# Up projection: five of 22 channel tiles from seven products of summed quarters, alternating with plain tiles

## The chip, the cores and the metric

One Trainium2 chip, and one of its cores. The metric is the device time of one execution in microseconds, the median of several runs of the same kernel.

## The reference, cut to what matters

A decoder layer: three attention branches are mixed and projected, and a gated MLP with a short convolution over positions follows. The change lies in the MLP's up projection alone.

```python
h = rmsnorm(x, norm_ffn_pre[l])                       # 512 tokens x 1024
u = causal_depthwise_conv(h @ w_ffn_up[l], ffn_conv_w[l], ffn_conv_b[l])   # 1024 x 5632
u_gate, u_val = jnp.split(u, 2, axis=-1)              # 2816 channels each
y = (jax.nn.gelu(u_gate, approximate=True) * u_val) @ w_ffn_down[l]
x = x + rmsnorm(y, norm_ffn_post[l])
```

Everything is float32. The kernel keeps that precision by splitting each operand into a high part and a low part in a rounded float32 format, and by three matmuls for each product (high x high, high x low, low x high).

## The kernel before, in words

The up projection makes 44 tiles of 128 channels x 512 tokens: for each f from 0 to 21 a gate tile (number 2f) and a value tile (number 2f+1). One tile is a sum over 8 slices of 128 inputs, and each slice takes the three matmuls of mm3 (lines 127 to 130), so a tile is 24 matmuls with 512 columns of moving data. The moving operands are h1h and h1l, the high and low parts of the normalized input, which stay in memory for the whole stage; the stationary operands are the weights.

Weights come in pieces of 128 partitions x 1024 values, one piece for a tile. issue (line 95) has SyncE load a piece into a raw buffer (line 103; four of them) and split (lines 81 to 88) makes its two parts: ScalarE copies raw to whi (line 84), and VectorE subtracts whi from raw to make wlo (line 85). There are three buffers each for whi and wlo; the loop asks for the piece of tile i+2 when tile i begins.

Each finished tile lies in a PSUM bank. conv (line 805) reads it three times: once on ScalarE (line 808) and twice on VectorE (lines 809 and 810), into one of four c buffers. The gate tile then goes through Gelu on ScalarE (line 822), and GpSimd multiplies gate and value (line 829). The down projection that follows already works with seven products of sums for 20 of the 22 tiles; after every fourth f sums (lines 783 to 790) makes its sums on GpSimd.

TensorE's instructions keep the order of the program. The other engines' order is set by a planner that simulates the program when it is built and gives an engine whichever instruction is ready, the earlier one of the program first; on the chip each engine then works through its list in that order. The four tiles 0 to 3 are begun early on half of the tokens (256 columns), which is why the trace of before has this shape too.

Of the kernel before, what the change touches and what calls it, by code (L numbers as in the profile page):

```python
# [11 lines left out]
F32 = mybir.dt.float32  # L12
F32R = mybir.dt.float32r
AF = mybir.ActivationFunctionType
ALU = mybir.AluOpType
# [4 lines left out]
P = 128  # L20
# [10 lines left out]
EARLY = 4  # L31
NG = 5
NS = 4 * NG
C_QMB, C_KMB, C_VMB, C_QSW, C_KSW, C_QME = 0, 512, 1024, 1536, 2048, 2304
C_GMB, C_GSW, C_GME = 2816, 3840, 4864

# [2 lines left out]
def tile_hybrid_layer(  # L39
# [24 lines left out]
    def T(pool_, shape, dt, tag, bufs=None):  # L64
        count[0] += 1
        kw = {} if bufs is None else {"bufs": bufs}
        return pool_.tile(shape, dt, tag=tag, name=f"{tag}_{count[0]}", **kw)

    def PT(tag):
        return T(pp, [P, 512], F32, tag, {"pj": 2, "s": 3, "t": 2, "o": 1}[tag])  # L70
# [24 lines left out]
    def issue(upto):  # L95

        while issued[0] <= min(upto, len(stream) - 1):
            i = issued[0]
            src, into = stream[i]
            k, c = src.shape[0] // P, src.shape[1]  # L100
            raw = T(wp, [P, 1024], F32, "raw", 4)
            view = raw[:].rearrange("p (k c) -> p k c", k=k)
            sp.dma_start(view, src.rearrange("(k p) c -> p k c", p=P))
            if into is None:
                dst = [(T(wp, [P, 1024], F32R, "whi", 3)[:], T(wp, [P, 1024], F32R, "wlo", 3)[:])]
            else:
                dst = into()
            hi, lo = [], []
            n = max(1, k // len(dst))
            for j, (a, b) in enumerate(dst):  # L110
                a3, b3 = (w.rearrange("p (k c) -> p k c", k=n) for w in (a, b))
                part = view[:, j * n : (j + 1) * n, :] if k > 1 else view[:, :, j * c // len(dst) : (j + 1) * c // len(dst)]
                split(a3, b3, part, eng=pool if i in on_pool else dve)
                hi += [a3[:, q, :] for q in range(n)]
                lo += [b3[:, q, :] for q in range(n)]
            units[i] = (hi, lo)
            issued[0] += 1
# [5 lines left out]
    def unit(i, ahead=2):  # L123
        issue(i + ahead)
        return units[i]
# [85 lines left out]
    def up_block(i, into=None):  # L211
        c = i // 2 + NF * (i % 2)
        b_up[i] = block(w_ffn_up[0][:, c * P : (c + 1) * P], into)
# [6 lines left out]
    up_block(0, lambda: [tuple(T(mp, [P, 1280], F32R, "P", 2)[:, 0:1024] for _ in range(2))])  # L220
    up_block(1, lambda: [tuple(T(ap, [P, 512], F32R, "pt", 5)[:] for _ in range(2)) for _ in range(2)])
    for i in range(2, 2 * NF):
        up_block(i)
    on_pool.update(b_mem[:3] + b_up[:3])


# [544 lines left out]
    fp = ctx.enter_context(tc.tile_pool(name="fp", bufs=2))  # L771
    c_tile = lambda: T(fp, [P, 512], F32, "c", 4)
    c_next = [c_tile()]
    gpair = [T(fp, [P, 4, 2, 256], F32, "G", NG) for _ in range(NG)]
    gsum = [[t[:, i, :] for i in range(3)] for t in (T(fp, [P, 3, 512], F32, "S", NG - 1) for _ in range(NG - 1))]
    gsum.append([T(mp, [P, 512], F32, "o", 3)[:] for _ in range(3)])
    grest = T(fp, [P, NF - NS, SEQ], F32, "gN", 1)

    def quarters(d):

# [11 lines left out]
    def up_products(i):  # L792

        if i in early:
            ps, u = early[i]
            a = 256
        else:
            u = unit(b_up[i])
            ps = PT("t" if i < EARLY + 2 else "pj")
            a = 0  # L800
        for k in range(KD):
            mm3(ps[:, a:512], u[0][k], u[1][k], h1h[:, k, a:512], h1l[:, k, a:512], k == 0, k == KD - 1)
            yield ps

    def conv(i, ps):
        ch = i // 2 + NF * (i % 2)
        c = c_next.pop() if c_next else c_tile()
        act.activation(c[:], ps[:], AF.Identity, scale=convw[:, 88 + ch : 89 + ch], bias=convw[:, 132 + ch : 133 + ch])  # L808
        dve.scalar_tensor_tensor(c[:, 1:512], ps[:, 0:511], convw[:, 44 + ch : 45 + ch], c[:, 1:512], op0=ALU.mult, op1=ALU.add)  # L809
        dve.scalar_tensor_tensor(c[:, 2:512], ps[:, 0:510], convw[:, ch : ch + 1], c[:, 2:512], op0=ALU.mult, op1=ALU.add)  # L810
        return c

    for f in range(NF):
        if f == 0:
            for k, banks in enumerate(zip(up_products(0), up_products(1))):
                if k + 4 < KD:
                    turn1(k + 4)
            issue(b_up[EARLY + 1])
        else:
            banks = [list(up_products(2 * f))[-1]]  # L820
        cg = conv(2 * f, banks[0])
        act.activation(cg[:], cg[:], AF.Gelu_apprx_tanh)  # L822
        if f:
            banks.append(list(up_products(2 * f + 1))[-1])
            issue(b_up[min(2 * f + 3, 2 * NF - 1)])
        cv = conv(2 * f + 1, banks[1])
        if f < NS:
            halves2 = lambda ap: ap.rearrange("p (c n) -> p c n", c=2)
            pool.tensor_tensor(gpair[f // 4][:, f % 2 :: 2, f % 4 // 2, :], halves2(cg[:]), halves2(cv[:]), op=ALU.mult)  # L829
        else:  # L830
            pool.tensor_tensor(grest[:, f - NS, :], cg[:], cv[:], op=ALU.mult)
        if f < NS and f % 4 == 3:
            sums(f // 4)

    gffn = [T(fp, [P, 512], F32, "gffn", 2) for _ in range(2)]
    for h in range(2):
# [198 lines left out]
```

## Time and profile before

| | us |
|---|---|
| median of 3 runs | 828.45 (828.23 to 828.81) |
| the profiled execution, its own time | 828.08 |
| its span, first to last instruction | 826.0 |
| up projection, first matmul of tile 4 to the first matmul of the down projection | 495.47 to 713.09 |

Times in the rows are microseconds from the start of the span, unless ns stands beside them. PE is TensorE's matmuls and PEld its weight loads, which overlap them; DVE is VectorE, ACT ScalarE, POOL GpSimd, SP SyncE. L85 is line 85 of the kernel. Matmuls are pipelined: one that is listed with 0.39 us makes room for the next 0.23 us after its own start, so the pace is read from the distance of starts. A group's row gives the count, the busy time, the mean ns of one, and the engine's idle time just before them with what ended it.

### The profile page before, as it was taken

What the parts mean: (1) busy time and instruction counts of PE and PEld (TensorE: products, weight loads), DVE (VectorE), ACT (ScalarE), POOL (GpSimd) and SP (SyncE); (2) the same over time, 40 slices, a digit from 0 to 9 for tenths busy, and PEclk for the clock granted to TensorE, in tenths of its full rate; (3) what the DMA queues carried; (4) which work ended last, traced back from release to release, by engine and by line L of the source; (5) the groups of instructions that cost most, each with busy time, mean ns of one, the idle gap of its engine ahead of it and who ended that gap; (6) DMA issues with size and microseconds to landing.
All of it is one profiled execution on the core that took longest, in us unless ns stands there. A gap on an engine that the chain in (4) does not pass through costs nothing.

```text
span 826.0 us, 10558 instructions
## 1 busy us (share of the span) xinstructions
PE 812.1 (98%) x3955; PEld 683.8 (83%) x3955; DVE 496.5 (60%) x825; ACT 399.3 (48%) x693; POOL 138.5 (17%) x117
## 2 busy tenths in 40 slices
PE   6999999999999999999999999999999999999996
PEld 6888888888888888888888898888888888888885
DVE  5846576667667665634564555444554445678775
ACT  6735555556656655432352444343343333567552
POOL 5000000000001010112213101414131413442301
PEclk9999999999999999999999999999999999999998
DMA  9732223323332233324354203333333333696922
GB/s 298 232 94 79 74 84 90 87 85 103 88 92 78 82 102 90 101 85 127 115 183 137 77 27 112 92 102 102 101 87 93 102 102 102 153 222 162 223 83 102
DMA packets 123121, 93.99 MB, mean 114 GB/s; under 512 B 3543, under 2 KB 107167, under 8 KB 123071
## 3 DMA queue, kind: packets, MB, share of 16 engines
q1 hardware_dynamic: 116287, 79.16, 32.1%
q0 software_dynamic: 6160, 13.11, 8.1%
q10 hardware_dynamic: 624, 1.06, 0.3%
q8 instruction: 31, 0.51, 0.2%
q14 instruction: 19, 0.16, 0.1%
HBM read 91.18 MB, written 2.14 MB: 113 GB/s over the span
## 4 chain that ended last, share of the span: by engine, by line
PE 96%; DMA 2%; SPq 1%; issue 1%; DVE 0%; ACT 0%; DVEq 0%; POOLq 0%; POOL 0%
PE pj L128 22%; PE pj L129 22%; PE pj L130 22%; PE t L461 2%; PE s L486 2%; PE s L923 2%; PE s L922 2%; PE s L924 2%; PE t L923 1%; PE t L922 1%; PE t L924 1%; PE o L470 1%; PE o L469 1%; PE o L923 1%; PE o L922 1%; PE o L924 1%
## 5 line engine op out<-in xcount | busy, mean ns | idle before, releaser
L128 PE MATMUL pj<-hT,whi 128*128 128x512 f32 (+1 forms) x704 | 273.8, 389 | 0.0
L129 PE MATMUL pj<-hT,whi 128*128 128x512 f32 (+1 forms) x704 | 271.0, 385 | 0.0
L130 PE MATMUL pj<-hT,wlo 128*128 128x512 f32 (+1 forms) x704 | 271.0, 385 | 0.0
L85 DVE TENSOR_TENSOR wlo<-raw,whi 128x1024 fp32r<-128x1024 f32 x127 | 164.2, 1294 | 176.4 <-ACT whi L84 176.3
L84 ACT ACTIVATE whi<-raw 128x1024 fp32r<-128x1024 f32 x131 | 138.5, 1058 | 172.5 <-PE pj L129 131.4
L130 PEld LDWEIGHTS pj<-hT,wlo 128*128 128x128 f32 x704 | 132.3, 188 | 26.5
L128 PEld LDWEIGHTS pj<-hT,whi 128*128 128x128 f32 x704 | 132.4, 188 | 24.5
L129 PEld LDWEIGHTS pj<-hT,whi 128*128 128x128 f32 x704 | 132.5, 188 | 24.2
L602 POOL TENSOR_TENSOR mx<-mx,gt 128x512 f32<-128x512 f32 x16 | 23.0, 1436 | 379.2 <-DVE gt L601 379.2
L829 POOL TENSOR_TENSOR G<-c,c 128x512 f32<-128x512 f32 x20 | 25.8, 1288 | 167.2 <-DVE c L810 149.4
L128 PE MATMUL pj<-oT,whi 128*128 128x512 f32 (+1 forms) x128 | 48.1, 376 | 0.0
L129 PE MATMUL pj<-oT,whi 128*128 128x512 f32 (+1 forms) x128 | 47.0, 367 | 0.0
L130 PE MATMUL pj<-oT,wlo 128*128 128x512 f32 (+1 forms) x128 | 46.9, 367 | 0.0
L84 ACT ACTIVATE pt<-t 128x512 fp32r<-128x512 f32 (+2 forms) x48 | 24.3, 543 | 36.9 <-PE t L461 36.8
L85 DVE TENSOR_TENSOR pt<-t,pt 128x512 fp32r<-128x512 f32 (+2 forms) x48 | 28.5, 621 | 20.0 <-ACT pt L84 19.5
L488 ACT ACTIVATE P<-P,tiny 128x256 f32<-128x256 f32 (+1 forms) x64 | 33.0, 517 | 14.0 <-DVE tiny L487 13.8
L822 ACT ACTIVATE c<-c 128x512 f32<-128x512 f32 x22 | 13.9, 632 | 42.9 <-DVE c L810 42.9
L810 DVE SCALAR_TENSOR_TENSOR c<-pj,convw,c 128x510 f32<-128x510 f32 x40 | 30.0, 750 | 1.4
L808 ACT ACTIVATE c<-pj,convw 128x512 f32<-128x512 f32 x40 | 30.4, 760 | 0.0
L809 DVE SCALAR_TENSOR_TENSOR c<-pj,convw,c 128x511 f32<-128x511 f32 x40 | 29.7, 743 | 0.0
L130 PEld LDWEIGHTS pj<-oT,wlo 128*128 128x128 f32 x128 | 24.6, 192 | 3.8
L128 PEld LDWEIGHTS pj<-oT,whi 128*128 128x128 f32 x128 | 24.6, 192 | 3.3
(346 smaller groups left out, 1284.6 us busy)
## 6 DMA issues: line engine op xcount, KB each, us to landing
raw<-in_w_in_dram SPq DMA_DIRECT2D x46, 512.0 KB, 3.9
raw<-in_w_ffn_up_dram SPq DMA_DIRECT2D x44, 512.0 KB, 3.9
hT<-in_w_ffn_down_dram POOLq DMA_DIRECT2D x13, 512.0 KB, 8.3
raw<-in_w_ffn_down_dram POOLq DMA_DIRECT2D x12, 512.0 KB, 8.2
raw<-in_w_mem_kv_dram SPq DMA_DIRECT2D x8, 512.0 KB, 5.9
raw<-in_w_out_dram SPq DMA_DIRECT2D x8, 512.0 KB, 3.3
raw<-in_w_ffn_down_dram SPq DMA_DIRECT2D x8, 512.0 KB, 3.4
mx<-in_x_dram SPq DMA_DIRECT2D x12, 256.0 KB, 4.9
```

The lines of the kernel that those rows point to most:

```text
L84: act.activation(hi, src, AF.Copy)
L85: eng.tensor_tensor(lo, src, hi.bitcast(F32), op=ALU.subtract)
L128: pe.matmul(ps, wh, xh, start=start, stop=False)
L129: pe.matmul(ps, wh, xl, start=False, stop=False)
L130: pe.matmul(ps, wl, xh, start=False, stop=stop)
L488: act.activation(dst, dst, AF.Exp, bias=mn[:, i : i + 1], scale=-1.0, accum_out=sm[:, i : i + 1])
L808: act.activation(c[:], ps[:], AF.Identity, scale=convw[:, 88 + ch : 89 + ch], bias=convw[:, 132 + ch : 133 + ch])
L809: dve.scalar_tensor_tensor(c[:, 1:512], ps[:, 0:511], convw[:, 44 + ch : 45 + ch], c[:, 1:512], op0=ALU.mult, op1=ALU.add)
L810: dve.scalar_tensor_tensor(c[:, 2:512], ps[:, 0:510], convw[:, ch : ch + 1], c[:, 2:512], op0=ALU.mult, op1=ALU.add)
L922: pe.matmul(ps[:], xh, wh, start=st, stop=False, skip_group_check=True)
L923: pe.matmul(ps[:], xh, wl, start=False, stop=False, skip_group_check=True)
L924: pe.matmul(ps[:], xl, wh, start=False, stop=end, skip_group_check=True)
```

## The change

For f = 5, 7, 9, 11 and 13 (SUP) the gate tile and the value tile are made together. Their weights are a matrix of 2 x 2 quarters (gate and value by the first and the second 512 inputs), the input is one too (the two halves of the inputs by the two halves of the tokens), and seven products of sums of quarters stand in for eight: the Winograd form of Strassen's scheme. One product (seventh) is 4 slices x 3 matmuls = 12 matmuls of 256 columns. Between the products stand the matmuls of the plain tiles of f+1, in four portions of 12 (steps), so that a product's operands and its PSUM bank have time.

input_sums makes the input's four sums once, in five portions during f = 0 to 4: eight operations of 1024 values, on VectorE and GpSimd, and eight splits of 512. They live in buffers that other stages leave idle here (rings xh, xl, op, gt, o and P), and the sums before their split in three G buffers; gpair, gsum and grest are taken from their rings later than before. fetch_up loads the two raw pieces of a SUP tile, weight_sums splits the first as it is and one half of the second (b22), and makes the four weight sums in place with four VectorE additions of 512 values; tile_pair splits both pieces again for the sums. The results are combined by four ScalarE copies and three VectorE operations of 256 columns into row_g and row_v in SBUF, which conv then reads in place of a PSUM bank. SUP's pieces are taken out of the stream of issue, and the calls of issue are placed by hand around the pairs. Tiles 6 and 7 take their PSUM banks from the ring s.

```diff
--- before.py
+++ after.py
@@ -31,6 +31,7 @@
 EARLY = 4
 NG = 5
 NS = 4 * NG
+SUP = (5, 7, 9, 11, 13)
 C_QMB, C_KMB, C_VMB, C_QSW, C_KSW, C_QME = 0, 512, 1024, 1536, 2048, 2304
 C_GMB, C_GSW, C_GME = 2816, 3840, 4864
 
@@ -220,7 +221,8 @@
     up_block(0, lambda: [tuple(T(mp, [P, 1280], F32R, "P", 2)[:, 0:1024] for _ in range(2))])
     up_block(1, lambda: [tuple(T(ap, [P, 512], F32R, "pt", 5)[:] for _ in range(2)) for _ in range(2)])
     for i in range(2, 2 * NF):
-        up_block(i)
+        if i // 2 not in SUP:
+            up_block(i)
     on_pool.update(b_mem[:3] + b_up[:3])
 
 
@@ -771,10 +773,52 @@
     fp = ctx.enter_context(tc.tile_pool(name="fp", bufs=2))
     c_tile = lambda: T(fp, [P, 512], F32, "c", 4)
     c_next = [c_tile()]
-    gpair = [T(fp, [P, 4, 2, 256], F32, "G", NG) for _ in range(NG)]
-    gsum = [[t[:, i, :] for i in range(3)] for t in (T(fp, [P, 3, 512], F32, "S", NG - 1) for _ in range(NG - 1))]
-    gsum.append([T(mp, [P, 512], F32, "o", 3)[:] for _ in range(3)])
-    grest = T(fp, [P, NF - NS, SEQ], F32, "gN", 1)
+    big_tile = lambda dt=F32: T(fp, [P, 2048], dt, "G", NG)[:]
+    gpair, gsum = {}, {}
+
+
+
+    parts = [big_tile().rearrange("p (a k c) -> p a k c", a=2, k=4) for _ in range(3)]
+    late = big_tile(F32R)
+    late_h, late_l = late[:, 0:1024], late[:, 1024:2048]
+    rows_s = T(fp, [P, 3, 512], F32, "S", NG - 1)
+    row_g, row_v = rows_s[:, 0, :], rows_s[:, 1, :]
+    p1_, u2_ = rows_s[:, 2, 0:256], rows_s[:, 2, 256:512]
+    p5_ = T(fp, [P, 512], F32, "gffn", 2)[:, 0:256]
+    b22 = T(fp, [P, 1024], F32R, "gN", 1)
+    b22 = [(b22[:, 0:512], b22[:, 512:1024])]
+    hsum = {}
+
+    def input_sums():
+
+        low, high = slice(0, 256), slice(256, 512)
+        quarter_in = {1: (slice(0, 4), low), 2: (slice(4, 8), low), 3: (slice(0, 4), high), 4: (slice(4, 8), high)}
+        a11, a21 = parts[0][:, 0], parts[0][:, 1]
+        a12, a22 = parts[1][:, 0], parts[1][:, 1]
+        s1, s2 = parts[2][:, 0], parts[2][:, 1]
+        for eng, q, dst in ((dve, 3, a21), (pool, 4, a22), (dve, 1, a11), (pool, 2, a12)):
+            k, c = quarter_in[q]
+            eng.tensor_tensor(dst, h1h[:, k, c].bitcast(F32), h1l[:, k, c].bitcast(F32), op=ALU.add)
+        yield
+        pool.tensor_tensor(s1, a21, a22, op=ALU.subtract)
+        dve.tensor_tensor(s2, s1, a11, op=ALU.subtract)
+        pool.tensor_tensor(a11, a11, a21, op=ALU.subtract)
+        pool.tensor_tensor(a12, a12, s2, op=ALU.add)
+        homes = [T(fp, [P, 512], F32R, tag, 3)[:] for tag in ("xh", "xl") for _ in range(3)]
+        homes += [T(mp, [P, 512], F32R, tag, n)[:] for tag, n in (("op", 2), ("gt", 2), ("o", 3)) for _ in range(n)]
+        for _ in range(2):
+            t = T(mp, [P, 1280], F32R, "P", 2)
+            homes += [t[:, 0:512], t[:, 512:1024]]
+        for j, src in ((2, s2), (1, s1), (3, a11), (4, a12)):
+            hsum[j] = []
+            for q in range(2):
+                hi, lo = (homes.pop(0).rearrange("p (k c) -> p k c", k=2) for _ in range(2))
+                split(hi, lo, src[:, 2 * q : 2 * q + 2, :])
+                hsum[j].append((hi, lo))
+            if j != 4:
+                yield
+        b22.append((homes.pop(0), T(fp, [P, 512], F32R, "gffn", 2)[:]))
+        yield
 
     def quarters(d):
 
@@ -795,14 +839,17 @@
             ps, u = early[i]
             a = 256
         else:
-            u = unit(b_up[i])
-            ps = PT("t" if i < EARLY + 2 else "pj")
+            if i < 2 * SUP[0]:
+                issue(min(b_up[i] + 2, b_up[2 * SUP[0] - 1]))
+            u = units[b_up[i]] if i < 2 * max(SUP) + 4 else unit(b_up[i])
+            ps = PT("t" if i < EARLY + 2 else "s" if i < EARLY + 4 else "pj")
             a = 0
         for k in range(KD):
             mm3(ps[:, a:512], u[0][k], u[1][k], h1h[:, k, a:512], h1l[:, k, a:512], k == 0, k == KD - 1)
             yield ps
 
     def conv(i, ps):
+        ps = ps[:]
         ch = i // 2 + NF * (i % 2)
         c = c_next.pop() if c_next else c_tile()
         act.activation(c[:], ps[:], AF.Identity, scale=convw[:, 88 + ch : 89 + ch], bias=convw[:, 132 + ch : 133 + ch])
@@ -810,7 +857,116 @@
         dve.scalar_tensor_tensor(c[:, 2:512], ps[:, 0:510], convw[:, ch : ch + 1], c[:, 2:512], op0=ALU.mult, op1=ALU.add)
         return c
 
-    for f in range(NF):
+    def gated(f, cg, cv):
+
+        if f < NS:
+            if f % 4 == 0:
+                gpair[f // 4] = T(fp, [P, 4, 2, 256], F32, "G", NG)
+            halves2 = lambda ap: ap.rearrange("p (c n) -> p c n", c=2)
+            pool.tensor_tensor(gpair[f // 4][:, f % 2 :: 2, f % 4 // 2, :], halves2(cg[:]), halves2(cv[:]), op=ALU.mult)
+        else:
+            pool.tensor_tensor(grest[:, f - NS, :], cg[:], cv[:], op=ALU.mult)
+        if f < NS and f % 4 == 3:
+            d = f // 4
+            if d < NG - 1:
+                t = T(fp, [P, 3, 512], F32, "S", NG - 1)
+                gsum[d] = [t[:, i, :] for i in range(3)]
+            else:
+                gsum[d] = [T(mp, [P, 512], F32, "o", 3)[:] for _ in range(3)]
+            sums(d)
+
+    def gate(i, bank):
+        cg = conv(i, bank)
+        act.activation(cg[:], cg[:], AF.Gelu_apprx_tanh)
+        return cg
+
+    def steps(gen, n):
+        for _ in range(n):
+            ps = next(gen)
+        return ps
+
+    def fetch_up(f):
+
+        raws = []
+        for c in (f, NF + f):
+            raw = T(wp, [P, 1024], F32, "raw", 4)[:]
+            sp.dma_start(raw.rearrange("p (k c) -> p k c", k=KD), w_ffn_up[0][:, c * P : (c + 1) * P].rearrange("(k p) c -> p k c", p=P))
+            raws.append(raw)
+        return raws
+
+    def wpair():
+        return T(wp, [P, 1024], F32R, "whi", 3)[:], T(wp, [P, 1024], F32R, "wlo", 3)[:]
+
+    def weight_sums(raws):
+
+        (g0, g1), (v0, v1) = ((r[:, 0:512], r[:, 512:1024]) for r in raws)
+        first = wpair()
+        split(*first, raws[0])
+        split(*b22[0], v1)
+        for dst, other in ((g0, v0), (v0, v1), (v1, g0), (g1, v1)):
+            dve.tensor_tensor(dst, dst, other, op=ALU.add)
+        return first
+
+    def seventh(ps, w, half, x, st):
+
+        wh, wl = (a[:, half * 512 : half * 512 + 512] for a in w)
+        for k in range(4):
+            c = slice(k * P, (k + 1) * P)
+            xh, xl = x(k)
+            pe.matmul(ps[:, 0:256], wh[:, c], xh, start=st and k == 0, stop=False, skip_group_check=True)
+            pe.matmul(ps[:, 0:256], wh[:, c], xl, start=False, stop=False, skip_group_check=True)
+            pe.matmul(ps[:, 0:256], wl[:, c], xh, start=False, stop=k == 3, skip_group_check=True)
+
+    def quarter_of(k0, c0):
+        return lambda k: (h1h[:, k0 + k, c0 : c0 + 256], h1l[:, k0 + k, c0 : c0 + 256])
+
+    def sum_of(j):
+        return lambda k: tuple(a[:, k % 2, :] for a in hsum[j][k // 2])
+
+    def tile_pair(f, raws, first):
+
+        more = f + 2 in SUP
+        w_22 = b22[0]
+        b22.reverse()
+        ng, nv = up_products(2 * f + 2), up_products(2 * f + 3)
+        w_v = wpair()
+        split(*w_v, raws[1])
+        split(late_h, late_l, raws[0])
+        by, bx = PT("t"), PT("s")
+        seventh(by, first, 0, quarter_of(0, 0), True)
+        act.activation(p1_, by[:, 0:256], AF.Copy)
+        seventh(bx, first, 1, quarter_of(4, 0), True)
+        dve.tensor_tensor(row_g[:, 0:256], bx[:, 0:256], p1_, op=ALU.add)
+        steps(ng, 4)
+        seventh(by, w_v, 1, sum_of(2), False)
+        act.activation(u2_, by[:, 0:256], AF.Copy)
+        issue(b_up[2 * f + 3])
+        bz = PT("s")
+        seventh(bz, (late_h, late_l), 0, sum_of(1), True)
+        act.activation(p5_, bz[:, 0:256], AF.Copy)
+        cg_n = gate(2 * f + 2, steps(ng, 4))
+        raws = fetch_up(f + 2) if more else None
+        seventh(by, w_v, 0, sum_of(3), False)
+        dve.tensor_tensor(row_v[:, 256:512], p5_, by[:, 0:256], op=ALU.subtract)
+        first = weight_sums(raws) if more else None
+        issue(b_up[2 * f + (6 if more else 4)])
+        steps(nv, 4)
+        seventh(bz, w_22, 0, sum_of(4), False)
+        dve.tensor_tensor(row_v[:, 0:256], bz[:, 0:256], u2_, op=ALU.subtract)
+        cv = conv(2 * f + 1, row_v)
+        seventh(by, (late_h, late_l), 1, quarter_of(4, 256), False)
+        act.activation(row_g[:, 256:512], by[:, 0:256], AF.Copy)
+        gated(f, gate(2 * f, row_g), cv)
+        gated(f + 1, cg_n, conv(2 * f + 3, steps(nv, 4)))
+        return raws, first
+
+    making = input_sums()
+    f = 0
+    while f < NF:
+        if f in SUP:
+            raws, first = tile_pair(f, raws, first)
+            f += 2
+            continue
         if f == 0:
             for k, banks in enumerate(zip(up_products(0), up_products(1))):
                 if k + 4 < KD:
@@ -818,19 +974,21 @@
             issue(b_up[EARLY + 1])
         else:
             banks = [list(up_products(2 * f))[-1]]
-        cg = conv(2 * f, banks[0])
-        act.activation(cg[:], cg[:], AF.Gelu_apprx_tanh)
+        cg = gate(2 * f, banks[0])
         if f:
             banks.append(list(up_products(2 * f + 1))[-1])
-            issue(b_up[min(2 * f + 3, 2 * NF - 1)])
-        cv = conv(2 * f + 1, banks[1])
-        if f < NS:
-            halves2 = lambda ap: ap.rearrange("p (c n) -> p c n", c=2)
-            pool.tensor_tensor(gpair[f // 4][:, f % 2 :: 2, f % 4 // 2, :], halves2(cg[:]), halves2(cv[:]), op=ALU.mult)
-        else:
-            pool.tensor_tensor(grest[:, f - NS, :], cg[:], cv[:], op=ALU.mult)
-        if f < NS and f % 4 == 3:
-            sums(f // 4)
+            if f + 1 in SUP:
+                raws = fetch_up(f + 1)
+                first = weight_sums(raws)
+                issue(b_up[2 * f + 4])
+            else:
+                issue(b_up[min(2 * f + 3, 2 * NF - 1)])
+        gated(f, cg, conv(2 * f + 1, banks[1]))
+        if f < SUP[0]:
+            next(making)
+        if f + 1 == NS:
+            grest = T(fp, [P, NF - NS, SEQ], F32, "gN", 1)
+        f += 1
 
     gffn = [T(fp, [P, 512], F32, "gffn", 2) for _ in range(2)]
     for h in range(2):
```

## Rows read from the trace of the kernel before

**Rows 1.** The page, its first part: busy time of an engine, its share of the span, and its instructions.

```profile
span 826.0 us, 10558 instructions
...
PE 812.1 (98%) x3955; PEld 683.8 (83%) x3955; DVE 496.5 (60%) x825; ACT 399.3 (48%) x693; POOL 138.5 (17%) x117
```

**Rows 2.** The page, its fourth part: the chain of work that ended last, shares of the span by engine.

```profile
PE 96%; DMA 2%; SPq 1%; issue 1%; DVE 0%; ACT 0%; DVEq 0%; POOLq 0%; POOL 0%
```

**Rows 3.** The table of stretches, one row for the up projection from tile 4 on: length, then the busy time (and instructions) of PE, PEld, DVE, ACT and POOL, the granted TensorE clock (1.00 is 2.4 GHz), the share of the DMA engines, GB/s.

```profile
495.47:713.09 217.62, 217.62 (x962) 180.19 (x961) 108.47 (x125) 84.63 (x107) 59.96 (x43) 1.00 0.34 97
```

**Rows 4.** Groups of TensorE instructions between 495 and 713 us: count, busy us and mean ns, and at the end the idle time before them.

```profile
L128 PE MATMUL pj<-hT,whi 128*128 128x512 f32 (+1 forms) x306 | 118.8, 388 | 0.0
```

**Rows 5.** TensorE in order of time, matmuls of 512 columns: start, length, line. The first is the first matmul of tile 4, the last the first of the down projection; between the two middle ones lie the three matmuls of one mm3.

```profile
495.47 0.40 PE L128 MATMUL t<-hT,whi 128*128 128x512 f32 x1
...
540.37 0.39 PE L128 MATMUL pj<-hT,whi 128*128 128x512 f32 x1
...
541.05 0.39 PE L128 MATMUL pj<-hT,whi 128*128 128x512 f32 x1
...
713.09 0.39 PE L922 MATMUL s<-whi,xh 128*128 128x512 f32 x1
```

**Rows 6.** TensorE in order of time, matmuls of 256 columns of the tiles begun early. 24 matmuls start from the first row up to the second, 47 more lie between the third and the one at 495.35.

```profile
473.57 0.28 PE L128 MATMUL s<-hT,pt 128*128 128x256 f32 x1
...
476.45 0.28 PE L128 MATMUL pj<-hT,whi 128*128 128x256 f32 x1
...
489.71 0.28 PE L128 MATMUL pj<-hT,whi 128*128 128x256 f32 x1
...
495.35 0.28 PE L130 MATMUL pj<-hT,wlo 128*128 128x256 f32 x1
```

**Rows 7.** TensorE where the width changes: from 512 columns to 256, and (after one of 128 columns) to 512.

```profile
206.74 0.39 PE L130 MATMUL pj<-hT,wlo 128*128 128x512 f32 x1
206.96 0.28 PE L469 MATMUL o<-pt,r 128*128 128x256 f32 x1
207.07 0.28 PE L470 MATMUL o<-pt,r 128*128 128x256 f32 x1
...
207.85 0.45 PE L128 MATMUL pj<-hT,whi 128*128 128x512 f32 x1
208.13 0.39 PE L129 MATMUL pj<-hT,whi 128*128 128x512 f32 x1
```

**Rows 8.** Groups of ScalarE and VectorE instructions between 482 and 713 us, shapes kept apart.

```profile
L84 ACT ACTIVATE whi<-raw 128x1024 fp32r<-128x1024 f32 x41 | 43.5, 1061 | 90.5 <-PE pj L129 85.8 <-PE t L129 3.3 <-issue 1.3
L808 ACT ACTIVATE c<-pj,convw 128x512 f32<-128x512 f32 x39 | 29.6, 760 | 0.0
L822 ACT ACTIVATE c<-c 128x512 f32<-128x512 f32 x22 | 13.9, 632 | 42.9 <-DVE c L810 42.9
L87 ACT ACTIVATE hT<-t,gam 128x256 fp32r<-128x256 f32 x4 | 1.9, 474 | 5.7 <-PE t L266 5.5
L84 ACT ACTIVATE xh<-G 128x512 fp32r<-128x512 f32 x3 | 1.8, 613 | 0.0
...
L85 DVE TENSOR_TENSOR wlo<-raw,whi 128x1024 fp32r<-128x1024 f32 x41 | 50.5, 1232 | 106.3 <-ACT whi L84 106.3
L810 DVE SCALAR_TENSOR_TENSOR c<-pj,convw,c 128x510 f32<-128x510 f32 x39 | 29.2, 750 | 1.4
L809 DVE SCALAR_TENSOR_TENSOR c<-pj,convw,c 128x511 f32<-128x511 f32 x39 | 29.0, 743 | 0.0
L85 DVE TENSOR_TENSOR xl<-G,xh 128x512 fp32r<-128x512 f32 x3 | 2.1, 684 | 0.0
L88 DVE SCALAR_TENSOR_TENSOR hT<-t,gam,hT 128x256 fp32r<-128x256 f32 x4 | 1.9, 484 | 3.7 <-ACT hT L87 3.6
```

**Rows 9.** VectorE in order of time: a weight split and the next instruction, and two instructions with both inputs in SBUF one after the other.

```profile
475.58 0.75 DVE L714 SCALAR_TENSOR_TENSOR mx<-op,tiny,mx 128x512 f32<-128x512 f32 x1
476.25 0.75 DVE L714 SCALAR_TENSOR_TENSOR mx<-gt,tiny,mx 128x512 f32<-128x512 f32 x1
...
567.28 1.23 DVE L85 TENSOR_TENSOR wlo<-raw,whi 128x1024 fp32r<-128x1024 f32 x1 [2.77 <-ACT whi L84]
568.42 0.74 DVE L809 SCALAR_TENSOR_TENSOR c<-pj,convw,c 128x511 f32<-128x511 f32 x1
```

**Rows 10.** GpSimd: groups between 482 and 713 us, then single instructions of GpSimd and VectorE that met.

```profile
L829 POOL TENSOR_TENSOR G<-c,c 128x512 f32<-128x512 f32 x20 | 25.8, 1288 | 167.2 <-DVE c L810 149.4 <-ACT c L822 17.8
L788 POOL TENSOR_TENSOR S<-S,G 128x512 f32<-128x512 f32 x4 | 9.0, 2261 | 0.3
...
L787 POOL TENSOR_TENSOR S<-G 128x512 f32<-128x512 f32 x4 | 5.2, 1295 | 0.3
...
567.39 2.26 POOL L788 TENSOR_TENSOR S<-S,G 128x512 f32<-128x512 f32 x1
...
496.47 1.30 POOL L829 TENSOR_TENSOR G<-c,c 128x512 f32<-128x512 f32 x1 [17.78 <-ACT c L822]
...
497.38 1.47 DVE L85 TENSOR_TENSOR wlo<-raw,whi 128x1024 fp32r<-128x1024 f32 x1 [0.90 <-ACT whi L84]
```

**Rows 11.** DMA issues between 480 and 713 us: count, KB each, median us from issue to landing.

```profile
raw<-in_w_ffn_up_dram SPq DMA_DIRECT2D x35, 512.0 KB, 3.8
```

## The prediction

> **What bounds the kernel now.** I read the page's busy times first: TensorE is busy for 98% of the span, VectorE for 60% [rows 1]. Busy TensorE may still be waiting work in disguise, so the chain that ended last comes next: 96% of it is TensorE itself [rows 2]. In the stage that the change touches, tiles 4 to 43 of the up projection, TensorE is busy for all of 217.62 us at the granted clock 1.00, the 2.4 GHz level [rows 3], and its matmuls have an idle time of 0.0 before them [rows 4]. VectorE has half of that stretch free, ScalarE 60% of it [rows 3]. So here matmul time is kernel time, one for one, until another engine comes too late.
>
> **The price of a matmul.** The stage's 40 tiles are 960 matmuls, from 495.47 to 713.09 [rows 5]: 217.62 / 960 = 0.2267 us each, which the three matmuls from 540.37 to 541.05 confirm (0.68 / 3). With 256 columns, 24 take 473.57 to 476.45, and 48 take 489.71 to 495.47 (the first start in rows 5): 0.120 us each [rows 6]. Half the columns thus cost 53% of the time: each matmul carries about 0.0133 us (2 x 0.120 - 0.2267) that doesn't shrink.
>
> **What is removed and added on TensorE.** A SUP pair was 2 x 24 matmuls of 512 columns, 48 x 0.2267 = 10.88 us. It becomes 7 x 12 = 84 of 256 columns, 84 x 0.120 = 10.08 us. The scheme saves an eighth of the columns (1.36 us), and the fixed part takes 0.56 back. Five pairs: 5 x 0.80 = 4.0 us. The order changes the width eight times in each pair, four times to 512 columns; a change from 512 to 256 costs nothing in the trace (206.74, 206.96, 207.07: pace 0.22 and then 0.11), one to 512 after a 128-column matmul 0.05 us (0.28 in place of 0.23) [rows 7], one to 512 after 256 columns nothing (495.35 to 495.47 is 0.12, and the tile is on pace). I take 0 and keep 5 x 4 x 0.05 = 1.0 us as the upper end, 0 as the lower.
>
> By the Trainium skill, "TensorE: Matmul & The Clock Gate", "Back-to-back issue gap", a matmul of N columns would take N / 2.4 + 2.5 ns, 109 and 216 ns. By it, as an estimate, a pair would save 10.4 - 9.2 = 1.2 us, and the time would be 822.5. The trace has 120 and 227 ns for these shapes, and the measurement decides.
>
> **What the other engines get.** Rows by piece: a split of 1024 values is 1.06 us on ScalarE and 1.23 on VectorE, one of 512 is 0.61 and 0.68, conv is 0.76 on ScalarE and 0.74 + 0.75 on VectorE, Gelu is 0.63, a 256-column operation from PSUM 0.47 and 0.48 [rows 8]. A SUP tile has three splits of 1024, one of 512, four additions of 512 (taken at the 0.68 of the 512 split's subtraction), three VectorE combinations, four ScalarE copies and two convs. VectorE: 3.7 + 0.7 + 2.7 + 1.4 + 3.0 = 11.5 us; with the plain tile's 2 x 1.23 + 2.98 = 5.4 it has 17 us of work in a pair of 10.08 + 10.88 = 20.96 us, 81% where it was 50%. ScalarE: 3.8 + 1.9 + 1.5 + 0.6 = 7.8, with the plain 4.3 is 12.1, 58%. Neither is the bound by volume. DMA moves the same bytes. GpSimd keeps its multiplications (1.29) and sums.
>
> **Does TensorE ever wait?** I laid the pair out by the prices above, with time 0 at its first product. Products end at 1.44 and 2.88, the gate tile's first half at 5.60, products three and four at 7.04 and 8.48, the gate's second half at 11.20, product five at 12.64, the value's first half at 15.36, products six and seven at 16.80 and 18.24, the value's second half at 20.96. Combinations have 2.7 us or more before their bank is written again. Raw pieces can be fetched once the last split that reads their buffer is done (about 5 us into the pair) and land 3.8 us later [rows 11], before the 11.0 at which the whi buffer for the next pair comes free. The tight place is the next pair's third product at 20.96 + 5.60 = 26.56: its weights (w_v) go to the whi buffer that the plain value tile holds until 20.8, so ScalarE's copy ends at about 22 and VectorE's half stands behind a queue. Start to start, VectorE takes 1.14 for a split of 1024, 1.53 for a conv from PSUM, and 0.67 for an operation of 512 with both inputs in SBUF [rows 9], so 1.34 for a conv from row_g or row_v; 0.6 for an addition is my estimate from the split's 1.14 for twice as much. From 12.05, when its first piece can be ready: split 13.2, conv of the gate tile 14.7, combination 15.2, four additions 17.6, split of the next plain piece 18.7, combination 19.2, split for product four 20.3, conv of row_v 21.7, conv of row_g 23.0, conv of the value tile 24.55, w_v from 24.55 or, if the multiplication of GpSimd stands in its way, 24.95, done at 26.1. It is in time by 0.45 us, on a queue without a gap. This place comes four times (the first pair has a plain tile before it). I take 0.1 us for each, 0.4 in all, from the lower end 0 and the upper end that the rivals give.
>
> **Before and after the pairs.** The input's sums (3 VectorE operations of 1024, 5 on GpSimd at twice 1.29 or so, eight splits of 512) fall in f = 0 to 4, some 54 us in which VectorE is half idle; a weight piece there is split one tile and more before its use (its copy begins when a buffer comes free, two tiles ahead), so 1 to 3 us of delay hide in that cover. If it were gone, each late piece would cost its delay. From f = 15 on, seven plain f (76 us) separate the pairs from the down projection, so that stage only moves forward. The buffers that the sums borrow are free again at f = 15.
>
> **Sum.** Against the profiled execution: 828.08 - 4.0 + 0.4 = 824.5. The median of before lies 0.37 above it, so 824.8.
>
> **What speaks against it.** GpSimd and VectorE block each other. GpSimd's L788 takes 2.26 us where its neighbour L787 takes 1.29: at 567.39 it starts just after VectorE's weight split (567.28 to 568.51, rows 9) and stands until that is over; and a split that meets a multiplication already running takes 1.47 in place of 1.23 [rows 8, 10]. The convs that read PSUM keep their 0.74 while L788 runs.
>
> The Trainium skill, "SBUF — State Buffer", "Who interferes with whom", has it as a lock: a VectorE instruction with two inputs in SBUF and a GpSimd instruction that reads SBUF exclude each other for their whole length. The rows agree for subtractions; that it holds for conv's form with SBUF inputs no row shows. The rule speaks against this change, which gives VectorE some 12 us of such instructions in a pair where two f had 4.9.
>
> **Rivals.**
> 1. The w_v piece comes late by one more GpSimd operation (1.29 us, rows 10) in each of four places: 1.29 - 0.45 = 0.84, 3.4 us in all. For it: no gap in the queue; against: on VectorE only some of it meets GpSimd. It gives 828.45 - 4.0 + 3.4 = 827.8, no change that can be measured (the measurement can tell about 0.2%, 1.7 us).
> 2. Slower: the exclusion makes VectorE the bound. After f = 7 and f = 11 GpSimd has six operations in a row, 7.7 us; if each holds VectorE up, a pair has 15.8 (by the distances above) + 7.7 = 23.5 us of VectorE time for 20.96 of TensorE, 2.5 late, in two pairs, and 0.84 in the two others: 6.7 - 4.0 = +2.7, 831.1. It decides once VectorE is held up by more than 0.45 + 1.0 us in each of the four pairs. Against: in that stretch (2 to 10 us of a pair) VectorE's other work is light.
> 3. The fixed 0.0133 us of a matmul doesn't come with these operands: 84 x 0.1067 = 8.96 against 10.88 saves up to 9.6 us, 819. The rows in this very shape speak against it [rows 6].
> 4. The gain is eaten in part by width changes at their upper end: 824.4 + 1.0, with some waiting 826.
>
> **How the numbers follow.** Forecast (waits under 2 us in all, 824.2 to 826.4) 0.66; rival 1 0.14; rival 2 0.09; rival 3 0.03; rival 4 0.08. Faster by over 0.2% (under 826.8): 0.66 + 0.03 + 0.08 = 0.77; within 0.2%: 0.14; slower: 0.09. The range of 8 in 10 goes from 824.0, the saving without any wait and a little, to 828.2, rival 1 with a margin; it leaves out rivals 2 and 3 and a little more.
>
> **What would show it.** Each step right: 256-column matmuls at 0.120 us in the seven products; the pairs 20.96 us apart; the down projection starts 3.6 to 4.0 us earlier; VectorE near 80% in the pairs; no wait of TensorE but a few tenths at the third product. Wrong: TensorE waiting for wlo or late parts at the third or fourth product (rivals 1 and 2), VectorE's two-input instructions longer than in rows 8, above all after f = 7 and 11, or a 512-column matmul after a product that starts later than 0.12 us.

## The result: 0.7% slower, and the profile after

| | before | changed |
|---|---|---|
| median, us | 828.48 (6 runs, 827.88 to 828.81) | 834.24 (6 runs, 834.09 to 834.38) |
| profiled execution, its span | 826.0 | 832.2 |
| tile 4 to the first matmul of the down projection | 495.47 to 713.09 | 495.96 to 718.77 |

The ratio is 1.007, 95% interval 1.0057 to 1.0083. The forecast was 824.8 and faster.

The page of the changed kernel, its first and fourth part, against [rows 1, 2]:

```profile
span 832.2 us, 11008 instructions
...
PE 810.8 (97%) x4135; PEld 690.6 (83%) x4135; DVE 546.6 (66%) x881; ACT 416.7 (50%) x731; POOL 162.6 (20%) x122
...
PE 91%; DVE 4%; issue 2%; POOL 1%; ACT 1%; DMA 1%; SPq 0%; DVEq 0%; POOLq 0%; ACTq 0%
```

TensorE's share of the chain has gone from 96% to 91%, and VectorE, which had 0% of the chain of before, has 4% of it. So the place to look is where the chain leaves TensorE. The table of stretches cuts the stage in three (columns as in [rows 3]): from tile 4 to the end of the first pair's fourth product, from there to the end of the last pair's seventh product, and what follows it.

```profile
495.96:545.90 49.94, 43.31 (x206) 36.00 (x205) 45.69 (x43) 22.83 (x34) 32.35 (x14) 0.97 0.29 85
545.90:639.86 93.96, 93.96 (x590) 85.11 (x589) 73.22 (x92) 48.51 (x72) 27.30 (x16) 1.00 0.36 105
639.86:718.77 78.91, 78.91 (x350) 65.33 (x349) 39.80 (x46) 30.69 (x40) 25.04 (x18) 1.00 0.36 98
```

Only the first stretch has TensorE idle (43.31 of 49.94 us busy), and there VectorE is busy for 45.69 of the 49.94. The second is gapless. The pairs' first products, in order of time:

```profile
529.69 0.28 PE L916 MATMUL t<-hT,whi 128*128 128x256 f32 x1
...
558.45 0.28 PE L916 MATMUL t<-hT,whi 128*128 128x256 f32 x1
...
579.49 0.28 PE L916 MATMUL t<-hT,whi 128*128 128x256 f32 x1
...
600.53 0.28 PE L916 MATMUL t<-hT,whi 128*128 128x256 f32 x1
...
621.57 0.28 PE L916 MATMUL t<-hT,whi 128*128 128x256 f32 x1
```

The last four lie 21.04 us apart, three times over: two f took 21.76 before (217.62 / 20 x 2), so a pair saves 0.72 us, and all five 3.6. This is the gain that was wanted. What ate it is in the list of TensorE's waits in the stage (total, times, longest) and in its order of time:

```profile
PE pj L129 <- DVE c L857: 4.1, 1, 4.1
PE s L918 <- DVE G L86: 1.8, 1, 1.8
PE pj L131 <- DVE wlo L86: 0.7, 1, 0.7
```

```profile
532.44 0.28 PE L918 MATMUL s<-hT,wlo 128*128 128x256 f32 x1
536.78 0.77 PE L129 MATMUL pj<-hT,whi 128*128 128x512 f32 x1 [4.06 <-DVE c L857]
537.34 0.63 PE L130 MATMUL pj<-hT,whi 128*128 128x512 f32 x1
...
539.48 0.47 PE L129 MATMUL pj<-hT,whi 128*128 128x512 f32 x1
...
542.48 0.28 PE L917 MATMUL s<-xl,G 128*128 128x256 f32 x1
544.61 0.39 PE L918 MATMUL s<-xl,G 128*128 128x256 f32 x1 [1.84 <-DVE G L86]
```

Between the matmuls at 532.44 and 536.78 TensorE stands before tile 12, the plain gate tile between the first pair's products, for its PSUM bank: VectorE's second conv instruction of tile 8 (L857), which frees it, ends only at 536.6. After this wait six matmuls are 0.42 to 0.56 us apart in place of 0.23, which costs 1.34 us more (536.78 to 539.48, less 6 x 0.2267). The granted clock of the stretch:

```profile
536.78:539.48 2.70, 2.70 (x7) 2.12 (x8) 1.15 (x2) 2.70 (x5) 0.77 (x1) 0.50 0.60 176
```

0.50 is the 1.2 GHz level: after it had stood, TensorE ran at it for 2.7 us. Then it waits again, from 542.48 to 544.61, for the low part of the fourth product's weights (late).

The sum: tiles 4 to 9 take 1.07 us more than before, most of it the wait for wlo in tile 8; the first pair takes 28.76 us (529.69 to 558.45), 7.72 more than the others; five pairs save 3.6. That is +5.2 us in the stage, 222.81 against 217.62. The rest of the 6.2 us of span lies at the start (tile 4 begins 0.49 us later) and at the end (last matmul to the end of the span, 7.58 against 7.05). A second profile of the unchanged kernel (below) shows 0.27 and 0.33 more at these two places, so about half of that or more can be variation.

What VectorE, GpSimd and ScalarE did before that wait, in order of time, first VectorE:

```profile
496.11 3.45 DVE L801 TENSOR_TENSOR G<-hT,hT 128x1024 f32<-128x1024 f32 x2
...
500.14 2.76 DVE L86 TENSOR_TENSOR wlo<-raw,whi 128x1024 fp32r<-128x1024 f32 x1
...
504.26 1.98 DVE L86 TENSOR_TENSOR wlo<-raw,whi 128x1024 fp32r<-128x1024 f32 x1
...
508.53 2.31 DVE L804 TENSOR_TENSOR G<-G,G 128x1024 f32<-128x1024 f32 x1 [1.62 <-POOL G L803]
...
511.42 2.46 DVE L86 TENSOR_TENSOR op<-G,op 128x512 fp32r<-128x512 f32 x1
513.81 2.89 DVE L86 TENSOR_TENSOR xh<-G,xh 128x512 fp32r<-128x512 f32 x1
...
517.83 1.21 DVE L86 TENSOR_TENSOR wlo<-raw,whi 128x1024 fp32r<-128x1024 f32 x1
...
529.62 3.36 DVE L907 TENSOR_TENSOR raw<-raw,raw 128x512 f32<-128x512 f32 x2
532.91 2.28 DVE L86 TENSOR_TENSOR wlo<-raw,whi 128x1024 fp32r<-128x1024 f32 x1
535.11 0.74 DVE L856 SCALAR_TENSOR_TENSOR c<-pj,convw,c 128x511 f32<-128x511 f32 x1
535.88 0.75 DVE L857 SCALAR_TENSOR_TENSOR c<-pj,convw,c 128x510 f32<-128x510 f32 x1
```

```profile
505.13 3.37 POOL L803 TENSOR_TENSOR G<-G,G 128x1024 f32<-128x1024 f32 x1
...
510.92 2.41 POOL L805 TENSOR_TENSOR G<-G 128x1024 f32<-128x1024 f32 x1 [1.16 <-DVE G L804]
513.30 2.85 POOL L806 TENSOR_TENSOR G<-G,G 128x1024 f32<-128x1024 f32 x1
521.70 3.95 POOL L866 TENSOR_TENSOR G<-c,c 128x512 f32<-128x512 f32 x1 [5.56 <-DVE c L857]
```

```profile
508.53 0.63 ACT L85 ACTIVATE op<-G 128x512 fp32r<-128x512 f32 x1 [5.40 <-POOL G L803]
```

VectorE's subtraction for 512 values takes 2.46 and 2.89 us where it takes 0.68 alone [rows 8], one for 1024 values 1.98 to 2.76 in place of 1.21 to 1.23, and the addition at 508.53 first waits 1.62 us for GpSimd's L803 and then takes 2.31. GpSimd's sums of 1024 values take 2.41 to 3.37, and the multiplication at 521.70, behind a row of VectorE's splits, 3.95 where it took 1.29 [rows 10]. These are the meetings of [rows 10], in a crowd. ScalarE, which copies the high part of a sum before VectorE subtracts it, stands 5.40 us for L803 as well, and its next conv (514.12) stands behind that copy.

### The profile page after: what moved, and what is told of

Same layout as the page of the kernel before. It is cut to its first block, busy times and chain, and to the rows that moved or that the text cites. A ratio compares the mean times of both kernels' runs of the same rounds, so it can differ in the third digit from the quotient of the medians.

```text
span 832.2 us, 11008 instructions
## 1 busy us (share of the span) xinstructions
PE 810.8 (97%) x4135; PEld 690.6 (83%) x4135; DVE 546.6 (66%) x881; ACT 416.7 (50%) x731; POOL 162.6 (20%) x122
## 4 chain that ended last, share of the span: by engine, by line
PE 91%; DVE 4%; issue 2%; POOL 1%; ACT 1%; DMA 1%; SPq 0%; DVEq 0%; POOLq 0%; ACTq 0%
PE pj L129 19%; PE pj L130 19%; PE pj L131 19%; PE t L463 2%; PE s L488 2%; PE s L1081 2%; PE s L1080 2%; PE s L1082 2%; PE t L1081 1%; PE t L1080 1%; PE t L1082 1%; PE o L472 1%; PE t L918 1%; PE t L917 1%; PE t L916 1%
## 5 line engine op out<-in xcount | busy, mean ns | idle before, releaser
L86 DVE TENSOR_TENSOR wlo<-raw,whi 128x1024 fp32r<-128x1024 f32 x127 | 168.8, 1330 | 125.3 <-ACT whi L85 125.2
L129 PE MATMUL pj<-hT,whi 128*128 128x512 f32 (+1 forms) x608 | 237.5, 391 | 4.1 <-DVE c L857 4.1
L131 PE MATMUL pj<-hT,wlo 128*128 128x512 f32 (+1 forms) x608 | 234.3, 385 | 0.7 <-DVE wlo L86 0.7
L130 PE MATMUL pj<-hT,whi 128*128 128x512 f32 (+1 forms) x608 | 234.4, 385 | 0.0
L129 PEld LDWEIGHTS pj<-hT,whi 128*128 128x128 f32 x608 | 114.9, 189 | 24.4 <-issue 4.2
L131 PEld LDWEIGHTS pj<-hT,wlo 128*128 128x128 f32 x608 | 114.5, 188 | 24.3 <-DVE wlo L86 1.1
L130 PEld LDWEIGHTS pj<-hT,whi 128*128 128x128 f32 x608 | 114.9, 189 | 19.8
L866 POOL TENSOR_TENSOR G<-c,c 128x512 f32<-128x512 f32 x20 | 33.5, 1677 | 146.5 <-ACT c L880 88.0
L129 PEld LDWEIGHTS pj<-oT,whi 128*128 128x128 f32 x128 | 24.7, 193 | 3.3
L130 PEld LDWEIGHTS pj<-oT,whi 128*128 128x128 f32 x128 | 24.6, 192 | 3.3
L1080 PE MATMUL s<-whi,xh 128*128 128x512 f32 x70 | 27.2, 389 | 0.0
L1081 PE MATMUL s<-wlo,xh 128*128 128x512 f32 x70 | 27.2, 389 | 0.0
```

Of the source, the lines that this page charges most:

```text
L86: eng.tensor_tensor(lo, src, hi.bitcast(F32), op=ALU.subtract)
L129: pe.matmul(ps, wh, xh, start=start, stop=False)
L130: pe.matmul(ps, wh, xl, start=False, stop=False)
L131: pe.matmul(ps, wl, xh, start=False, stop=stop)
L1080: pe.matmul(ps[:], xh, wh, start=st, stop=False, skip_group_check=True)
L1081: pe.matmul(ps[:], xh, wl, start=False, stop=False, skip_group_check=True)
```

## The experiments

Three theories stood at the start. A: GpSimd and VectorE exclude each other while the input's sums are made, VectorE's list falls behind, and the banks with it. B: VectorE simply has too much to do before the first pair. C: the first pair's weight sums stand ahead of convs in VectorE's list. D, added with the second group of runs: what counts is that VectorE waits in order for GpSimd's results. Each run is compared with the kernel before on its own chip: 828.75 us for the first four, 828.42 for the others.

### All input sums on VectorE

```diff
-        for eng, q, dst in ((dve, 3, a21), (pool, 4, a22), (dve, 1, a11), (pool, 2, a12)):
+        for eng, q, dst in ((dve, 3, a21), (dve, 4, a22), (dve, 1, a11), (dve, 2, a12)):
...
-        pool.tensor_tensor(s1, a21, a22, op=ALU.subtract)
+        dve.tensor_tensor(s1, a21, a22, op=ALU.subtract)
...
-        pool.tensor_tensor(a11, a11, a21, op=ALU.subtract)
-        pool.tensor_tensor(a12, a12, s2, op=ALU.add)
+        dve.tensor_tensor(a11, a11, a21, op=ALU.subtract)
+        dve.tensor_tensor(a12, a12, s2, op=ALU.add)
```

> All eight operations that make the input's sums run on VectorE; the rest is the changed kernel. Theory A (exclusion: while the sums are made during f = 0 to 4, GpSimd's five instructions of 1024 values and VectorE's instructions with two SBUF inputs hold each other up, 1.2 us becomes 2.3 to 3, the convs fall behind, and TensorE waits for a PSUM bank): the meeting is gone, VectorE's instructions return to 1.14 to 1.23 us, the wait of 4.1 us before tile 12 is gone or under 1.5 us, time 825 to 828. Theory B (volume: VectorE simply has too much to do before the first pair, whoever it meets): five more instructions of 1.14 us on VectorE, waits grow by up to 5.7 us, time 836 to 840. Theory C (order: the first pair's weight sums stand ahead of the convs in VectorE's list): about as now, 833 to 836.

Measured: 830.47 us, ratio 1.0016 (1.0007 to 1.0026). VectorE got five instructions more, and the kernel became 4.0 us faster, each against its own reference (+1.7 where the changed kernel has +5.8). That rules out B and C by themselves. But the time lies above A's range. The ten runs fall into two groups, three at 828.59 to 828.97 us with a mean granted clock of 0.999 and seven at 829.89 to 831.16 with 0.995 to 0.997. The profile is of one at 828.87: it has no wait for the bank and two others in the first pair, and what TensorE waited for in the seven is not shown.

```profile
PE s L918 <- DVE G L86: 2.7, 1, 2.7
PE t L918 <- DVE wlo L86: 0.4, 1, 0.4
```

VectorE has no gap in this profile (third figure):

```profile
495.00:536.00 41.00, 40.63 (x200) 34.30 (x199) 41.00 (x47) 23.29 (x32) 14.74 (x8) 1.00 0.27 77
```

So volume can count too, though not as B had it: eight sums on VectorE still cost 3.6 us against no sums at all (826.90 on the same chip, below).

### All input sums on GpSimd

Two lines: pool in place of dve in the list of the first four operations, and for s2, so that all eight run on GpSimd.

> All eight operations that make the input's sums run on GpSimd. Theory A: more of GpSimd's long instructions to meet, time 834 to 840. Theory B: VectorE has 3 x 1.14 = 3.4 us less to do, time 829 to 832. Theory C: about as now, 833 to 836.

Measured: 833.98 us, ratio 1.0065 (1.005 to 1.008). 3.4 us of VectorE's work are gone and nothing is won, against B. The time is C's, and A's range began at 834; A and C are not told apart by it. Against the run without sums, which gives VectorE the same work, the sums cost 7.1 us here, meeting and dependence together: ScalarE stands 3.7 and 3.4 us for GpSimd's sums. VectorE's weight splits (1024 values) and one input split (the last, 512 values) in this run, with no wait of VectorE for a sum among them:

```profile
504.01 2.54 DVE L86 TENSOR_TENSOR wlo<-raw,whi 128x1024 fp32r<-128x1024 f32 x1 [1.72 <-ACT whi L85]
...
519.16 2.32 DVE L86 TENSOR_TENSOR wlo<-raw,whi 128x1024 fp32r<-128x1024 f32 x1
...
524.22 2.88 DVE L86 TENSOR_TENSOR xl<-G,xh 128x512 fp32r<-128x512 f32 x1
```

### No input sums

```diff
-        for eng, q, dst in ((dve, 3, a21), (pool, 4, a22), (dve, 1, a11), (pool, 2, a12)):
+        s2, s1, a11, a12 = (h1h[:, k, c].bitcast(F32) for k, c in (quarter_in[j] for j in (4, 3, 1, 2)))
+        for eng, q, dst in ():
```

The s1, s2, a11 and a12 operations and the three buffers for the sums go too.

> The eight input sums are left out (the four products that take a sum take one plain quarter of the input in its place, so the five pairs' output is not the reference's); their splits, all weight sums and all products stay. Theory A: GpSimd has nothing long to do before the first pair, no wait of TensorE, time 824.5 to 826. Theory B: only 3.4 us less on VectorE, time 829 to 832. Theory C: weight sums still stand ahead of the convs, waits stay above 3 us, 830 to 835.

Measured: 826.90 us, ratio 0.9979 (0.9969 to 0.9988): faster than before, below the ranges of B and C and 0.9 us above A's. One wait is left, 1.5 us inside the first pair's fourth product. VectorE at that place, and GpSimd's instruction that it met there:

```profile
522.44 3.37 DVE L901 TENSOR_TENSOR raw<-raw,raw 128x512 f32<-128x512 f32 x2
525.73 2.31 DVE L86 TENSOR_TENSOR wlo<-raw,whi 128x1024 fp32r<-128x1024 f32 x1
...
533.98 1.22 DVE L86 TENSOR_TENSOR wlo<-raw,whi 128x1024 fp32r<-128x1024 f32 x1
535.11 2.31 DVE L86 TENSOR_TENSOR G<-raw,G 128x1024 fp32r<-128x1024 f32 x1
```

```profile
534.20 2.13 POOL L860 TENSOR_TENSOR G<-c,c 128x512 f32<-128x512 f32 x1 [3.76 <-DVE c L851]
```

The additions, the split at 525.73 and the one at 535.11, whose result TensorE waits for, are again at 1.7 and 2.3 us: GpSimd works on the down projection's sums after f = 3 (from 523.6) and multiplies at 534.20.

### The pairs begin at f = 7

```diff
-SUP = (5, 7, 9, 11, 13)
+SUP = (7, 9, 11, 13, 15)
...
-            next(making)
+            next(making, None)
```

> The five pairs begin at f = 7 in place of 5 (7, 9, 11, 13, 15), with the same operations on the same engines; the first pair's weights come 22 us later, the input's sums keep their places. Theories A and B: what falls behind in f = 0 to 4 is caught up in two more plain tiles' time, waits under 2 us in all, time 824.5 to 827. Theory C: the wait moves with the first pair, still 4 us and more, 831 to 835.

Measured: 831.86 us, ratio 1.0044 (1.0027 to 1.006). The number is C's; the range that A and B share is missed by 5 us. The mechanism isn't C's: the first pair, now at f = 7, runs without a wait, and the waits for the banks come at about the same time as in the changed kernel, ahead of tiles 10 and 11, which are now plain tiles, with no weight sum near them.

```profile
PE pj L129 <- DVE c L857: 3.8, 2, 3.2
```

So A needed mending: the sums on two engines stop TensorE with the pairs at f = 5 and at f = 7, and starting the pairs later gives back 2.65 us of 5.76, not all.

### Sums that nobody uses

VectorE makes three and GpSimd five sums, each from data of its own; the splits take plain quarters, as in the run without sums.

```diff
-        pool.tensor_tensor(s1, a21, a22, op=ALU.subtract)
-        dve.tensor_tensor(s2, s1, a11, op=ALU.subtract)
-        pool.tensor_tensor(a11, a11, a21, op=ALU.subtract)
-        pool.tensor_tensor(a12, a12, s2, op=ALU.add)
+        pool.tensor_tensor(s1, a12, a22, op=ALU.subtract)
+        dve.tensor_tensor(s2, a21, a11, op=ALU.subtract)
+        pool.tensor_tensor(a22, a22, a12, op=ALU.subtract)
+        pool.tensor_tensor(a12, a12, s1, op=ALU.add)
+        s2, s1, a11, a12 = (h1h[:, k, c].bitcast(F32) for k, c in (quarter_in[j] for j in (4, 3, 1, 2)))
```

> As the run without input sums (the four products take plain quarters, so the five pairs' output is not the reference's), but VectorE still does three and GpSimd five operations of 1024 values on the same buffers, each engine on data of its own, and nobody uses the results. Theory A (exclusion of GpSimd and VectorE): VectorE's instructions are held up as in the changed kernel although nothing depends on GpSimd, they take 2.3 to 3 us where they meet, waits of TensorE of 4 us and more, time 830 to 835. Theory D (dependence: VectorE stands in order behind GpSimd's results): as without the sums plus 3 x 1.14 us on VectorE that has room, 827 to 829.

Measured: 830.66 us, ratio 1.0029 (1.0018 to 1.0039). Without a single dependence between the two engines' sums the time rises by 4.1 us over the run without sums (+2.2 against -1.9), to A's range and not D's. A's waits of 4 us and more did not come. The one wait stands where the run without sums has its own, and is 1.4 us longer:

```profile
PE s L919 <- DVE G L86: 2.9, 1, 2.9
```

Most of the rest are matmuls after it at the lower clock (granted 0.50 from 541.48 to 543.61). VectorE, then GpSimd:

```profile
502.37 3.37 DVE L804 TENSOR_TENSOR G<-G 128x1024 f32<-128x1024 f32 x1
505.66 3.42 DVE L86 TENSOR_TENSOR wlo<-raw,whi 128x1024 fp32r<-128x1024 f32 x1
```

```profile
502.25 5.76 POOL L801 TENSOR_TENSOR G<-hT,hT 128x1024 f32<-128x1024 f32 x2
508.08 3.26 POOL L803 TENSOR_TENSOR G<-G 128x1024 f32<-128x1024 f32 x1
```

A subtraction and a split of 1024 values take 3.37 and 3.42 us next to GpSimd's sums. So A's meeting comes without D's dependence, 2.2 us for each of the two. But VectorE's three sums are added work as well, some 3.4 us, so the 4.1 us are not shown to be the meeting's alone. The changed kernel stands 3.5 us higher still; there dependence comes on top (VectorE's 1.62 us before 508.53), and the order of the list differs too, so this remainder is not divided further.

### Without the down projection's sums after f = 3

As the run without input sums, and in sums:

```diff
+        if d == 0:
+            gsum[0] = [a11, a12, a22]
+            return
         pool.tensor_tensor(s1, a21, a22, op=ALU.subtract)
```

> As the run without input sums, and GpSimd's four sums for the down projection after f = 3 are left out too (that group takes plain quarters; the output is not the reference's). Theory A: the last wait, 1.5 us at the first pair's fourth product, came from VectorE meeting GpSimd's row of instructions from f = 3 on, and is gone or under 0.5 us; time 1.2 to 1.8 us below the run without sums, that is 3.3 us or so below the kernel before. Theory B (volume of VectorE's work before the first pair): no change, the wait of 1.5 us stays.

Measured: 825.52 us, ratio 0.9963 (0.9949 to 0.9976), 2.9 us below the kernel before. That is 1.05 us below the run without input sums, a little less than the 1.2 to 1.8 expected. VectorE's work is the same as in that run, and the last wait has all but gone, as A had it and B had not:

```profile
PE s L915 <- DVE G L86: 0.2, 1, 0.2
```

### Later pairs, and all sums on VectorE

The first and the fourth edit together; nothing is left out.

> The five pairs begin at f = 7 (7, 9, 11, 13, 15) and all eight input sums run on VectorE. Theory A: nothing long on GpSimd to meet, and two more plain f before the first pair: no wait of TensorE over 0.3 us in the stage, 5 x 0.72 us saved, faster than before by 2.5 to 3.6 us (ratio 0.9957 to 0.997). Theory B: VectorE has 11 f of work more evenly, but waits of 2 us and more stay around f = 3 and 4, ratio 0.999 to 1.003.

Measured: 825.67 us (5 runs, 825.55 to 826.02), ratio 0.9966 (0.9952 to 0.9979): 2.75 us faster than the kernel before and 8.5 faster than the change as it was made (each against its own reference), in A's range. The stage, and its only wait:

```profile
495.84:710.44 214.60, 214.31 (x1142) 185.43 (x1141) 154.38 (x186) 102.85 (x145) 68.06 (x43) 1.00 0.36 101
```

```profile
PE pj L129 <- DVE c L857: 0.3, 1, 0.3
```

214.60 us against 217.62: 5 x 0.72 saved, less 0.6. VectorE has five instructions more in the stage than in the changed kernel (186 against 181) and is busy for less, 154.38 us against 158.71. Neither edit does this by itself (830.47 and 831.86).

### The kernel before, once more

> The kernel before, unchanged, for a second profile: how far the start (first loads, before the first matmuls) and the end (last matmul to the end of the span) vary by themselves. If the 0.5 us that the changed kernels show more at each of the two belongs to the change, this run shows 495.5 us to tile 4 and 7.05 us at the end; if it is variation, up to 0.5 us more at either.

Measured: span 826.6, tile 4 at 495.74, 7.38 us from the last matmul to the end. The stage itself repeats to 0.04 us:

```profile
495.74:713.40 217.66, 217.66 (x963) 180.22 (x962) 108.50 (x125) 84.67 (x107) 59.95 (x43) 1.00 0.34 97
```

So about half of what the changed kernel showed more at start and end is seen without the change; the other 0.2 us at each is not settled.

## Why the prediction was wrong

- **The price of a pair** was right in kind and a tenth too high: 0.72 us for 0.80. The 256-column matmuls keep their 0.120 us; each portion of 12 wide ones takes 2.75 in place of 2.72, somewhat over half the 0.05 that I gave as the upper end for a change of width. The formula from the Trainium skill, "TensorE: Matmul & The Clock Gate", "Back-to-back issue gap", is given there for an isolated matmul and not for a stream. Its 1.2 us for a pair, an estimate, did not come.
- **The tight place in the pairs** (third product, 0.45 us to spare) held, with VectorE ahead of the plan: the four later pairs have no wait at all, with VectorE busy for 78% of that stretch (73.22 of 93.96), as 81% was forecast. Rival 1 did not come true. The rows show more to spare than forecast: by the order of ScalarE's copies the split for w_v is the one at 560.86, over 2.0 us before the second pair's third product begins.

```profile
560.86 1.22 DVE L86 TENSOR_TENSOR wlo<-raw,whi 128x1024 fp32r<-128x1024 f32 x1
...
564.07 0.28 PE L916 MATMUL t<-xh,whi 128*128 128x256 f32 x1
```

- **The step that failed** is the one called "Before and after the pairs". It took VectorE to be "half idle" in f = 0 to 4 and let "1 to 3 us of delay hide" in the cover of the weight pieces. The trace shows VectorE busy for 45.69 of 49.94 us from tile 4 into the first pair, because its instructions with two SBUF inputs and GpSimd's stretch each other, VectorE's to up to four times their length. The window was too long as well: f = 0 to 4 were put at "some 54 us", but f = 0 and 1 are the tiles begun early, and from VectorE's first sum (496.11) to the first pair (529.69) there are 33.6. And the cover that ran out was not that of the weight pieces, on which TensorE waited only 0.7 us in the tiles before the pairs, but above all that of the PSUM banks, which the late convs held (4.1 us, and 1.3 at the lower clock behind it); 1.8 more went to the late weight sum of the fourth product.
- **Rival 2** had the mechanism, the exclusion making VectorE the bound, and the sign, but half the size (+2.7 against +5.8, of which 1.3 is the clock). It was placed after f = 7 and 11, where TensorE waits for nothing, and given 9%. I had the rows for it in hand [rows 10] and applied them to the pairs only. Five instructions of 2.4 us or more on GpSimd and eleven of VectorE, side by side in a few f, were priced by their lengths alone.
- The Trainium skill, "SBUF — State Buffer", "Who interferes with whom", says that a VectorE instruction with two SBUF inputs and a GpSimd instruction that reads SBUF exclude each other. The runs agree: the subtraction at 513.81 took 2.89 us for 0.68 and ended 0.55 after GpSimd's L806 (513.30 to 516.15), and one of 1024 values took 3.42 for 1.21 in the run with unused sums. Whether conv with SBUF inputs (c<-S) is held up as well no row here shows: none of them met a GpSimd instruction in the changed kernel, and they took 0.75.

Shown by runs: that the sums' place on GpSimd costs (+5.8 to +1.7 when they move to VectorE), that the meeting stretches VectorE's instructions without any dependence, that sums on VectorE alone cost too (3.6 us), and that the last wait comes from the sums after f = 3. Only argued: how much of the 4.1 us is the meeting and how much VectorE's three added sums, and how the remaining 3.5 us divide between dependence, order and clock.

## What to carry to other kernels

Work that "falls beside" a busy engine must be laid out against every engine that shares something with it, not only against its own idle time: first list who reads two SBUF operands at the same time as GpSimd works, in each stretch, the preparation included. Moving instructions from an idle engine to the busier one can be a gain: it was 4.0 us here, and with two more plain f before the first pair the change became worth 2.75 us. And one-time preparation deserves the same timeline as the steady state: the distance of the pairs, 20.96 us in the forecast, was 21.04.

## What the runs showed of the hardware that was not expected

- A wait of TensorE of 4.1 us cost more than itself: the next six matmuls ran at a granted clock of 0.50, the lower level, 1.34 us more.
- Instructions of the two engines do not just take turns with a small loss. In a crowd, a 512-value subtraction of VectorE took 2.46 and 2.89 us for 0.68, and a GpSimd multiplication, begun beside a row of VectorE's splits, 3.95 for 1.29.
